# Attention scores by pairs of heads, each head on 64 of TensorE's rows

## The chip, the cores and the metric

The kernel runs on one core of a Trainium2 chip. The metric is the time of one execution on the device, in microseconds (us). Before the change three runs gave a median of 867.17 us, between 867.12 and 867.3. Beside the runs there is one profiled execution, from which all durations below are taken.

The engines of the core are named as the profile names them: PE is TensorE (matmuls; PEld its weight loads, which overlap), DVE is VectorE, ACT is ScalarE, POOL is GpSimd, and SP only issues DMAs. TensorE writes its results to PSUM, eight banks of 512 float32 columns on 128 partitions; DVE and ACT read them from there.

## The reference

One layer of a hybrid encoder on a sequence of 512 frames with a model width of 1024: an RMS norm, one wide projection, an attention branch and a recurrent branch, a gated merge, a SwiGLU feed-forward part and a final norm, all in float32. Only the attention branch is touched here. It has 16 heads of 64 features:

```python
q, k, v = ...                       # 512 x 1024 each, columns of xn @ w_in
s = einsum('bnqhd,bnkhd->bhnqk', q, kb) * (1 / 8)
s = s + rel_bias_band(rel_table)    # per head, on the clipped relative distance
s = where(valid, s, -1e30)          # chunks of 64 frames, own chunk and the 8 before it
p = softmax(s)
o = einsum('bhnqk,bnkhd->bnqhd', p, vb)
ya = o @ w_attn_out
```

With 512 frames there are eight chunks, so the band of nine chunks means: each frame sees its own chunk of 64 and everything before it.

## The kernel before

**Products in parts.** Every float32 operand x is kept as a high part (fp32r, written by ACT with a copy) and a low part (x minus the high part, written by DVE): `split`, line 80. A projection multiplies by `mm3`, line 74: high by high, high by low, low by high, three matmuls into one PSUM bank. `project` (line 342) does this for the eight slices of 128 of the contraction, so one tile of 128 output features by 512 frames is 24 matmuls.

**PSUM.** Three tags share the eight banks: `mm` has four, `s` two, `t` two. A tile of the program is one bank.

**Order.** Everything is traced in program order into a planner, which puts each engine's instructions in an order by its own simulation, and sets the semaphores from what each instruction reads and writes. Within `tc.manual_schedule(engines={PE})` (line 973) TensorE keeps the order in which the program names its instructions; DVE, ACT, POOL and SP are still ordered by the planner there. The loop over heads of the attention lies inside this block; the scores of the first head lie before it, among the products of `yb` (line 967 to 972).

**A pair's q and k.** Columns of w_in come in chunks `qk0` to `qk7`, 128 columns of q and 128 of k for a pair of heads, and `v0` to `v3` for four heads each. `q_tile` (line 834) projects q for a pair, features on partitions: head e of the pair has rows 64e to 64e+63. It writes the high part of the head into its own 64 rows of a tile and the low part into the other 64 rows (lines 841 and 842, for each head), so that a contraction over all 128 rows gives (high + low) times whatever stands in the 128 rows of the other operand. `k_tile` (line 845) makes two such operands for each head: the high part in both halves of the rows (lines 852 and 854) and the low part in both halves (853 by DVE, then a copy by POOL, 855).

**A head's scores** (`scores`, line 879). Frames are turned within blocks of 128, so that block qb of 128 queries needs the first (qb+1)*128 keys: 128, 256, 384 and 512 columns. `products(qb)` is two matmuls over 128 rows, q with the high part of k (line 895) and with the low part (896). Block 0 writes columns 0 to 127 and block 1 columns 256 to 511 of the same bank (`low`); blocks 2 and 3 have a bank each. In the program products(0) and products(1) both come before block 0 is read, products(2) before block 1 is read, and so on. Reading a block is line 904: DVE takes scores and bias from PSUM and SBUF, writes bias minus scores to SBUF and its minimum per row to `nmax` (the DVE_READ_ACCUMULATOR2 row beside it). ACT then takes the exponential with its row sum (905). The four reciprocals are one DVE instruction (906), and the four blocks are scaled by POOL, for three of the heads the last block by DVE (910).

**The other steps of a head.** `transposed` (913): ten 128 by 128 transposes by TensorE into three banks, which are split into high and low parts. `weigh` (930): eight matmuls of v with these, gathered into `oacc` by ACT and DVE (942, 943); after the second head of a pair the result is split into `aT`, the input of the projection `ya`.

**The loop** (lines 974 to 983) does, for head h: transposed(h), scores(h+1), a part of what is laid out by `laid(h)`, weigh(h), the rest of it. `laid` gives q and k of the pair after next, and v of the next four heads, in the order of the chunks; for the last four heads the products of `gate`. In the first iteration q and k of pair 1 come after scores(1), and are first used by scores(2) in the iteration after it.

Of the kernel before, what the change touches and what calls it, by code (L numbers as in the profile page):

```python
# [14 lines left out]
P = 128  # L15
# [23 lines left out]
def block_kernel(ctx: ExitStack, tc: tile.TileContext, x, norm_mix_g, w_in, b_merge, rel_table,  # L39
# [22 lines left out]
    qk_stack, qkp = opened("qk", 3, "right")  # L62
# [455 lines left out]
    def junk_of(pl, tag, bufs, name):  # L518
        return pl.tile([P, D], F32, tag=tag, bufs=bufs, name=f"junk_{name}")

    def rstds(half):

        q = cp.tile([P, 4], F32, tag="ssq", bufs=4, name=f"ssq{half}")
        sd = cp.tile([P, 2], F32, tag="sd", bufs=4, name=f"sd_mix{half}")
        rs = cp.tile([P, 2], F32, tag="rs", bufs=4, name=f"rs_mix{half}")
        a, b = xt[2 * half], xt[2 * half + 1]
        junk = junk_of(nm, "junk", 1, f"a{half}")
        act.activation(junk[:], a[:], AF.Square, accum_out=q[:, 0:1])
        act.activation(sd[:, 0:1], q[:, 0:1], AF.Sqrt, bias=eps_t[:], scale=1.0 / D)
# [3 lines left out]
        junk = junk_of(qkp, "qk", 3, f"c{half}")  # L533
# [287 lines left out]
    def backwards(ap):  # L821
        return blocks(ap)[:, :, ::-1]

    def halves(e):
        own, other = slice(e * HD, e * HD + HD), slice(HD - e * HD, 2 * HD - e * HD)
        return own, other


    qk = {}

    def qk_pool(pr):
        return aw if pr % 2 else qkp

    def q_tile(pr):
        po = mm_tile(f"po_q{pr}")
        project(po, weights(f"qk{pr}"), 0, xnT)
        q = qk_pool(pr).tile([P, 2, S], F32R, tag="qk", bufs=3, name=f"q{pr}")
        for e in range(2):
            own, other = halves(e)
            src = backwards(po[own, :])  # L840
            act.activation(blocks(q[own, e]), src, AF.Copy, scale=0.125)
            dve.scalar_tensor_tensor(blocks(q[other, e]), src, 0.125, blocks(f(q[own, e])), ALU.mult, ALU.subtract)
        qk[pr] = [q]

    def k_tile(pr):
        po = mm_tile(f"po_k{pr}")
        project(po, weights(f"qk{pr}"), 1, xnT)
        kh = qk_pool(pr).tile([P, 2, S], F32R, tag="qk", bufs=3, name=f"kh{pr}")
        kl = qk_pool(pr).tile([P, 2, S], F32R, tag="qk", bufs=3, name=f"kl{pr}")
        for e in range(2):  # L850
            own, other = halves(e)
            act.activation(kh[own, e], po[own, :], AF.Copy)
            dve.tensor_sub(kl[own, e], po[own, :], f(kh[own, e]))
            act.activation(kh[other, e], po[own, :], AF.Copy)
            pool.tensor_copy(kl[other, e], kl[own, e])
        qk[pr] += [kh, kl]

    q_tile(0)
    k_tile(0)
# [16 lines left out]
        vs.setdefault(gr, []).append(v)  # L876


    def scores(h):
        pr, e = divmod(h, 2)  # L880
        q, kh, kl = qk[pr]
        bias = bias_tile(h)
        lsum = cp.tile([P, NT], F32, tag="lsum", bufs=2, name=f"l{h}")
        nmax = cp.tile([P, NT], F32, tag="nmax", bufs=2, name=f"m{h}")
        rl = cp.tile([P, NT], F32, tag="rl", bufs=2, name=f"rl{h}")
        prob = [aw2.tile([P, (qb + 1) * P], F32, tag=f"p{qb}", name=f"p{h}_{qb}") for qb in range(NT)]

        low = ps.tile([P, S], F32, tag="s", bufs=2, name=f"s{h}_01")
        scs = [low[:, 0:P], low[:, 256:512], mm_tile(f"s{h}_2"), ps.tile([P, S], F32, tag="s", bufs=2, name=f"s{h}_3")]

        def products(qb):
            w = (qb + 1) * P
            sc = scs[qb][:, 0:w]
            qs = q[:, e, qb * P:(qb + 1) * P]
            pe.matmul(sc, qs, kh[:, e, 0:w], start=True, stop=False, skip_group_check=qb < 2)
            pe.matmul(sc, qs, kl[:, e, 0:w], start=False, stop=True, skip_group_check=qb < 2)  # L896

        products(0)
        for qb in range(NT):
            w = (qb + 1) * P  # L900
            if qb < NT - 1:
                products(qb + 1)

            dve.tensor_tensor_reduce(prob[qb][:], scs[qb][:, 0:w], bias[:, S - w:S], -1.0, 3e38, ALU.add, ALU.min, nmax[:, qb:qb + 1])  # L904
            act.activation(prob[qb][:], prob[qb][:], AF.Exp, bias=nmax[:, qb:qb + 1], scale=-1.0, accum_out=lsum[:, qb:qb + 1])  # L905
        dve.reciprocal(rl[:], lsum[:])  # L906
        for qb in range(NT):

            eng = dve if qb == NT - 1 and h % 4 == 1 and h > 1 else pool
            eng.tensor_scalar(prob[qb][:], prob[qb][:], rl[:, qb:qb + 1], 1.0, ALU.mult, ALU.mult)  # L910
        return prob

    def transposed(h, prob):

        pp = [aw2.tile([P, 2, S], F32R, tag="pt", bufs=4, name=f"pp{h}_{i}") for i in range(3)]
        for i, kbs in enumerate(((0,), (1,), (2, 3))):
            pt = mm_tile(f"pT{h}_{i}") if i == 2 else ps.tile([P, S], F32, tag="t", bufs=2, name=f"pT{h}_{i}")
            for kb in kbs:
                for qb in range(kb, NT):
                    at = qb - min(kb, 2) if kb < 3 else 2  # L920
                    pe.transpose(pt[:, at * P:(at + 1) * P], prob[qb][:, kb * P:(kb + 1) * P], ident[:])  # L921
            n = (512, 384, 384)[i]
            split(pp[i][:, 0, 0:n], pp[i][:, 1, 0:n], pt[:, 0:n])
        return pp

    aT = []
    aT_pairs = []
    oacc = []

    def weigh(h, pp):  # L930
        pr, e = divmod(h, 2)
        own, other = halves(e)
        if e == 0:
            oacc.append(tg_.tile([P, S], F32, tag="tg", name=f"oacc{pr}"))
        acc = oacc[pr]
        po = mm_tile(f"o{h}")
        for kb in range(NT):
            i, lo, n = ((0, 0, 512), (1, 0, 384), (2, 0, 256), (2, 256, 128))[kb]
            st = vs[pr // 2][kb][:, pr % 2, 2 * e:2 * e + 2].rearrange("p a d -> p (a d)")
            for part in range(2):  # L940
                pe.matmul(po[:, S - n:S], st, pp[i][:, part, lo:lo + n], start=kb == 0 and part == 0, stop=kb == NT - 1 and part == 1)  # L941
        act.activation(acc[own, :], po[other, :], AF.Copy)
        dve.tensor_add(acc[own, :], po[own, :], acc[own, :])
        if e == 1:
            if pr % 2 == 0:
                aT_pairs.append(rnp.tile([P, 2, 2, S], F32R, tag="big", bufs=4, name=f"aT{pr}"))
            o = aT_pairs[-1][:, pr % 2]
            split(blocks(o[:, 0]), blocks(o[:, 1]), backwards(acc[:]))
            aT.append(o)

    def laid(h):
        m, at = divmod(h, 4)
        qs, ks, va = (lambda pr: lambda: q_tile(pr)), (lambda pr: lambda: k_tile(pr)), (lambda t: lambda: v_tile(m + 1, t))
        if h >= 12:
            return [lambda: gate(0, h - 8)], []
        first_, second = 2 * m + 2, 2 * m + 3
        return {0: (([qs(1), ks(1)] if m == 0 else []) + ([] if m == 0 else [qs(first_)]), [qs(first_)] if m == 0 else []),
                1: ([ks(first_)], [va(0)]),  # L960
                2: ([va(1), va(2)], [va(3)]),
                3: ([qs(second)], [ks(second)])}[at]

    for t in range(NT):
        v_tile(0, t)
# [5 lines left out]
        project(po, weights(f"yb{j - j % 2}"), j % 2, rnn)  # L971
        dve.scalar_tensor_tensor(zB[j], zB[j], 1.0, po[:], ALU.add, ALU.mult)
    with tc.manual_schedule(engines={mybir.EngineType.PE}):
        for h in range(HEADS):
            pp = transposed(h, prob)
            if h + 1 < HEADS:
                prob = scores(h + 1)
            before, after = laid(h)
            for what in before:
                what()  # L980
            weigh(h, pp)
            for what in after:
                what()
    aw2_stack.close()
    wo_stack, wop = opened("wo", 4)
    extra["wo1"] = wop
# [373 lines left out]
```

## Time and profile before

| what | value |
|---|---|
| median of three runs | 867.17 us |
| span of the profiled execution, first to last instruction | 865.5 us |
| PE busy | 856.4 us, 99% of the span |
| DVE busy | 600.9 us, 69% |
| ACT busy | 498.1 us, 58% |
| POOL busy | 95.2 us, 11% |
| mean granted clock of TensorE | 0.998 |
| DMA | 96.39 MB, mean 111 GB/s |

The profiled execution has no time of its own beside its span; the median lies 1.67 us above it, for what lies ahead of the first and behind the last instruction.

How to read the rows: a row of a timeline gives the start in us from the start of the span, the duration in us, the engine, the line of the program, the operation, the tiles as out<-in, the shape, and how many instructions were merged (x1 is one). In brackets stands how long the engine had been idle before it, and what ended that. Matmuls overlap: each lasts longer than the distance to the next one's start, and it is this distance that adds up to the time of TensorE. A row that groups instructions gives their busy time and the mean duration of one in ns. A row of waits gives who waited for whom, the sum in us, how often, and sometimes the longest.

### The profile page before, as it was taken

Reading aid. Unit: us, or ns where it says so; the run is one execution under the profiler, and the core shown is the slowest. Engines: PE = TensorE matmul, PEld = TensorE weight load, DVE = VectorE, ACT = ScalarE, POOL = GpSimd, SP = SyncE. Lnnn points to the kernel's source line nnn. Section 1 sums busy time; section 2 is a strip of 40 time slices with the busy share of each in tenths; the row PEclk is TensorE's granted clock in tenths of the full one; section 3 lists DMA queues with packets and bytes.
Section 4 is the critical chain, followed back from the end, with each engine's and each line's share of the span. In section 5 each row is a group of like instructions: output and inputs, shape, how many; then the busy total and the mean of one; then the engine's idle time right before and its main releaser. Section 6 shows DMA issues by size and latency. Waiting matters only on the chain.

```text
span 865.5 us, 13353 instructions
## 1 busy us (share of the span) xinstructions
PE 856.4 (99%) x5130; PEld 761.1 (88%) x5130; DVE 600.9 (69%) x950; ACT 498.1 (58%) x878; POOL 95.2 (11%) x161
## 2 busy tenths in 40 slices
PE   9999999999999999999999999999999999999997
PEld 6988888888889889898888889999999999888885
DVE  5666656573456585766556556988888888698885
ACT  6595747752356585767633357555555556545434
POOL 2412111120112132221200000000000001000000
PEclk9999999999999999999999999999999999999999
DMA  9133232433323332232223712424333332437542
GB/s 289 57 119 106 68 120 76 123 98 98 109 88 95 81 103 74 81 113 64 74 76 121 266 51 72 145 79 131 109 98 98 99 98 85 148 100 227 185 134 97
DMA packets 88767, 96.39 MB, mean 111 GB/s; under 512 B 5784, under 2 KB 74992, under 8 KB 88704
## 3 DMA queue, kind: packets, MB, share of 16 engines
q1 hardware_dynamic: 87072, 92.03, 34.3%
q10 hardware_dynamic: 1232, 2.95, 0.9%
q8 instruction: 40, 0.66, 0.3%
q0 software_dynamic: 400, 0.57, 0.2%
q14 instruction: 23, 0.19, 0.1%
HBM read 93.39 MB, written 2.14 MB: 110 GB/s over the span
## 4 chain that ended last, share of the span: by engine, by line
PE 97%; DVE 1%; ACT 1%; DMA 0%; issue 0%; ACTq 0%; DVEq 0%
PE po_out L76 2%; PE po_out L77 2%; PE po_out L78 2%; PE o L941 2%; PE p_fu L78 2%; PE p_fg L78 2%; PE p_fg L77 2%; PE p_fg L76 2%; PE p_fu L76 2%; PE p_fu L77 2%; PE pT L921 2%; PE po_v L76 2%; PE po_v L78 2%; PE po_v L77 2%; PE po_gb L76 2%; PE po_xr L77 2%
## 5 line engine op out<-in xcount | busy, mean ns | idle before, releaser
L910 POOL TENSOR_SCALAR p<-p,rl 128x128 f32<-128x128 f32 (+3 forms) x61 | 34.9, 590 | 135.7 <-DVE rl L906 135.4
L905 ACT ACTIVATE p<-p,m 128x128 f32<-128x128 f32 (+1 forms) x64 | 35.7, 560 | 11.0 <-DVE m L904 10.8
L76 PE MATMUL po_v<-whl_v,xnT 128*128 128x256 f32 x128 | 36.5, 285 | 0.0
L78 PE MATMUL po_v<-whl_v,xnT 128*128 128x256 f32 x128 | 36.2, 283 | 0.0
L77 PE MATMUL po_v<-whl_v,xnT 128*128 128x256 f32 x128 | 36.2, 283 | 0.0
L1131 POOL TENSOR_TENSOR act_lo<-act,act_hi 128x1024 fp32r<-128x1024 f32 x1 | 2.4, 2405 | 300.7 <-ACT act_hi L1130 300.7
L76 PE MATMUL po_out<-whl_fo,act_hi 128*128 128x512 f32 (+1 forms) x80 | 30.8, 385 | 0.5 <-ACT c_u L370 0.5
L78 PE MATMUL po_out<-whl_fo,act_lo 128*128 128x512 f32 (+1 forms) x80 | 30.7, 384 | 0.0
L77 PE MATMUL po_out<-whl_fo,act_hi 128*128 128x512 f32 (+1 forms) x80 | 30.7, 384 | 0.0
L904 DVE CUSTOM_DVE_ANT_0 p<-s,bias 128x128 f32<-128x128 f32 (+1 forms) x64 | 29.1, 483 | 1.0 <-PE s L896 1.0
L83 DVE TENSOR_TENSOR whl_qk<-raw_qk,whl_qk 128x1024 fp32r<-128x1024 f32 x16 | 20.5, 1284 | 13.2 <-ACT whl_qk L82 13.0
L83 DVE TENSOR_TENSOR whl_fu_s<-s_fu,whl_fu_s 128x1024 fp32r<-128x1024 f32 x20 | 24.1, 1222 | 6.2 <-ACT whl_fu_s L82 6.2
L77 PE MATMUL po_xr<-xnT,whl_xr 128*128 128x512 f32 (+1 forms) x80 | 27.7, 353 | 0.0
L83 DVE TENSOR_TENSOR pp<-pT,pp 128x384 fp32r<-128x384 f32 (+1 forms) x48 | 27.5, 596 | 0.1
L77 PE MATMUL po_gr<-xnT,whl_gr 128*128 128x512 f32 (+1 forms) x80 | 27.5, 347 | 0.0
L78 PE MATMUL po_gr<-xnT,whl_gr 128*128 128x512 f32 (+1 forms) x80 | 27.3, 347 | 0.0
L78 PE MATMUL po_xr<-xnT,whl_xr 128*128 128x512 f32 (+1 forms) x80 | 27.2, 346 | 0.0
L76 PE MATMUL po_gr<-xnT,whl_gr 128*128 128x512 f32 (+1 forms) x80 | 27.2, 347 | 0.0
L83 DVE TENSOR_TENSOR whl_fg_s<-s_fg,whl_fg_s 128x1024 fp32r<-128x1024 f32 x20 | 24.0, 1222 | 4.1 <-ACT whl_fg_s L82 4.0
L76 PE MATMUL po_xr<-xnT,whl_xr 128*128 128x512 f32 (+1 forms) x80 | 26.3, 351 | 0.4 <-ACT xnT L566 0.4
L82 ACT ACTIVATE whl_qk<-raw_qk 128x1024 fp32r<-128x1024 f32 x16 | 16.8, 1053 | 17.0 <-PE po_yb L78 10.4
L76 PE MATMUL po_gb<-xnT,whl_gb 128*128 128x512 f32 x64 | 25.2, 394 | 0.0
(487 smaller groups left out, 3247.5 us busy)
## 6 DMA issues: line engine op xcount, KB each, us to landing
raw_fg<-in_w_ffn_in_dram SPq DMA_DIRECT2D x24, 512.0 KB, 4.2
raw_fu<-in_w_ffn_in_dram SPq DMA_DIRECT2D x22, 512.0 KB, 3.9
raw_qk<-in_w_in_dram SPq DMA_DIRECT2D x32, 256.0 KB, 3.2
raw_fo<-in_w_ffn_out_dram SPq DMA_DIRECT2D x16, 512.0 KB, 3.6
raw_xr<-in_w_in_dram SPq DMA_DIRECT2D x8, 512.0 KB, 4.3
raw_gr<-in_w_in_dram SPq DMA_DIRECT2D x8, 512.0 KB, 3.6
raw_ga<-in_w_in_dram SPq DMA_DIRECT2D x8, 512.0 KB, 4.7
raw_gb<-in_w_in_dram SPq DMA_DIRECT2D x8, 512.0 KB, 3.5
```

Source lines behind the costliest of these rows:

```text
L76: pe.matmul(o, sh, mh, start=start, stop=False, skip_group_check=parts)
L77: pe.matmul(o, sh, ml, start=False, stop=False, skip_group_check=parts)
L78: pe.matmul(o, sl, mh, start=False, stop=stop, skip_group_check=parts)
L82: act.activation(hi, src, AF.Copy)
L83: dve.tensor_sub(lo, src, f(hi))
L904: dve.tensor_tensor_reduce(prob[qb][:], scs[qb][:, 0:w], bias[:, S - w:S], -1.0, 3e38, ALU.add, ALU.min, nmax[:, qb:qb + 1])
L905: act.activation(prob[qb][:], prob[qb][:], AF.Exp, bias=nmax[:, qb:qb + 1], scale=-1.0, accum_out=lsum[:, qb:qb + 1])
L910: eng.tensor_scalar(prob[qb][:], prob[qb][:], rl[:, qb:qb + 1], 1.0, ALU.mult, ALU.mult)
L921: pe.transpose(pt[:, at * P:(at + 1) * P], prob[qb][:, kb * P:(kb + 1) * P], ident[:])
L941: pe.matmul(po[:, S - n:S], st, pp[i][:, part, lo:lo + n], start=kb == 0 and part == 0, stop=kb == NT - 1 and part == 1)
L1131: (dve if i else pool).tensor_sub(lo[:], o[:], f(hi[:]))
```

## The change

A pair of heads is now one unit. The tile of q holds the high part of both heads (each on its own 64 rows) and, beside it, the low part; the tile of k likewise. No part is written twice any more, and POOL copies nothing. A head's product is three matmuls over its 64 rows: q high with k high, q high with k low, q low with k high. Those of head 0 (rows 0 to 63) and head 1 (rows 64 to 127) follow each other in turn, each head into a bank of its own. For a pair and a block there are six matmuls of 64 rows where there were four of 128.

The scores of a pair take six banks: `low` of both heads from tag `s`, `mid` (block 2) from `t`, `last` (block 3) from `mm`. In the program the order is now products(qb) and at once the reading of block qb for both heads, then products(qb+1). The loop runs over eight pairs: for pair pr it does scores(pr+1), q of pair pr+2 and one tile of v, transposed(pr) for both heads, k of pair pr+2 and one more tile of v, weigh(pr) for both heads. In its first iteration q and k of pair 1 come ahead of scores(1). Scaling by the reciprocal is left wholly to POOL. The tiles of q and k have two buffers instead of three, the probabilities four instead of two, and the transposed parts get tags of their own by size.

```diff
     def q_tile(pr):
         po = mm_tile(f"po_q{pr}")
         project(po, weights(f"qk{pr}"), 0, xnT)
-        q = qk_pool(pr).tile([P, 2, S], F32R, tag="qk", bufs=3, name=f"q{pr}")
-        for e in range(2):
-            own, other = halves(e)
-            src = backwards(po[own, :])
-            act.activation(blocks(q[own, e]), src, AF.Copy, scale=0.125)
-            dve.scalar_tensor_tensor(blocks(q[other, e]), src, 0.125, blocks(f(q[own, e])), ALU.mult, ALU.subtract)
+        q = qk_tile(pr, "q")
+        src = backwards(po[:])
+        act.activation(blocks(q[:, 0]), src, AF.Copy, scale=0.125)
+        dve.scalar_tensor_tensor(blocks(q[:, 1]), src, 0.125, blocks(f(q[:, 0])), ALU.mult, ALU.subtract)
         qk[pr] = [q]
 
     def k_tile(pr):
         po = mm_tile(f"po_k{pr}")
         project(po, weights(f"qk{pr}"), 1, xnT)
-        kh = qk_pool(pr).tile([P, 2, S], F32R, tag="qk", bufs=3, name=f"kh{pr}")
-        kl = qk_pool(pr).tile([P, 2, S], F32R, tag="qk", bufs=3, name=f"kl{pr}")
-        for e in range(2):
-            own, other = halves(e)
-            act.activation(kh[own, e], po[own, :], AF.Copy)
-            dve.tensor_sub(kl[own, e], po[own, :], f(kh[own, e]))
-            act.activation(kh[other, e], po[own, :], AF.Copy)
-            pool.tensor_copy(kl[other, e], kl[own, e])
-        qk[pr] += [kh, kl]
+        k = qk_tile(pr, "k")
+        split(k[:, 0], k[:, 1], po[:])
+        qk[pr].append(k)
...
-    def scores(h):
...
+    def scores(pr):
+        q, k = qk[pr]
+        bias = [bias_tile(2 * pr + e) for e in range(2)]
...
+        low = [ps.tile([P, S], F32, tag="s", bufs=2, name=f"s{pr}_{e}_01") for e in range(2)]
+        mid = [ps.tile([P, S], F32, tag="t", bufs=2, name=f"s{pr}_{e}_2") for e in range(2)]
+        last = [mm_tile(f"s{pr}_{e}_3") for e in range(2)]
+        scs = [[low[e][:, 0:P], low[e][:, 256:512], mid[e][:, 0:3 * P], last[e][:]] for e in range(2)]
 
         def products(qb):
             w = (qb + 1) * P
-            sc = scs[qb][:, 0:w]
-            qs = q[:, e, qb * P:(qb + 1) * P]
-            pe.matmul(sc, qs, kh[:, e, 0:w], start=True, stop=False, skip_group_check=qb < 2)
-            pe.matmul(sc, qs, kl[:, e, 0:w], start=False, stop=True, skip_group_check=qb < 2)
-
-        products(0)
+            at = slice(qb * P, (qb + 1) * P)
+            for n, (qp, kp) in enumerate(((0, 0), (0, 1), (1, 0))):
+                for e in range(2):
+                    rows = half_of(e)
+                    pe.matmul(scs[e][qb], q[rows, qp, at], k[rows, kp, 0:w], start=n == 0, stop=n == 2,
+                              skip_group_check=qb < 2)
+
+        def weighted(qb, e):
+            p, n = prob[e][qb], stat[e]
+            at = slice(qb, qb + 1)
+            dve.tensor_tensor_reduce(p[:], scs[e][qb], bias[e][:, S - (qb + 1) * P:S], -1.0, 3e38, ALU.add, ALU.min,
+                                     n["nmax"][:, at])
+            act.activation(p[:], p[:], AF.Exp, bias=n["nmax"][:, at], scale=-1.0, accum_out=n["lsum"][:, at])
+
         for qb in range(NT):
-            w = (qb + 1) * P
-            if qb < NT - 1:
-                products(qb + 1)
-
-            dve.tensor_tensor_reduce(prob[qb][:], scs[qb][:, 0:w], bias[:, S - w:S], -1.0, 3e38, ALU.add, ALU.min, nmax[:, qb:qb + 1])
...
+            products(qb)
+            for e in range(2):
+                weighted(qb, e)
...
+    def laid(pr):
+        if pr >= 6:
+            return [], [lambda: gate(0, 2 * pr - 8)], [lambda: gate(0, 2 * pr - 7)]
+        m, at = divmod(pr, 2)
+        qs, ks, va = (lambda p: lambda: q_tile(p)), (lambda p: lambda: k_tile(p)), (lambda t: lambda: v_tile(m + 1, t))
+        return ([qs(1), ks(1)] if pr == 0 else [], [qs(pr + 2), va(2 * at)], [ks(pr + 2), va(2 * at + 1)])
...
     with tc.manual_schedule(engines={mybir.EngineType.PE}):
-        for h in range(HEADS):
-            pp = transposed(h, prob)
-            if h + 1 < HEADS:
-                prob = scores(h + 1)
-            before, after = laid(h)
-            for what in before:
+        for pr in range(HEADS // 2):
+            first_, second, third = laid(pr)
+            for what in first_:
                 what()
-            weigh(h, pp)
-            for what in after:
+            ahead = scores(pr + 1) if pr + 1 < HEADS // 2 else None
+            for what in second:
                 what()
+            pp = transposed(pr, prob)
+            for what in third:
+                what()
+            weigh(pr, pp)
+            prob = ahead
```

More of the change, by code (lines that the diff above doesn't have):

```diff
@@ L822, in backwards, with half_of, qk_tile @@
         return blocks(ap)[:, :, ::-1]
[L824 to L826 removed]
+    def half_of(e):
+        return slice(e * HD, e * HD + HD)
     qk = {}
[L831 to L832 removed]
+    def qk_tile(pr, name):
+        return (aw if pr % 2 else qkp).tile([P, 2, S], F32R, tag="qk", bufs=2, name=f"{name}{pr}")
     def q_tile(pr):
@@ L926, in block_kernel @@
     aT = []
     aT_pairs = []
[L928 to L949, printed above, removed]
@@ L953, in laid, with weigh @@
[L953 to L962, printed above, removed]
+    def weigh(pr, pps):
+        acc = tg_.tile([P, S], F32, tag="tg", name=f"oacc{pr}")
+        for e, pp in enumerate(pps):
+            own, other = half_of(e), half_of(1 - e)
+            po = mm_tile(f"o{pr}_{e}")
+            for kb in range(NT):
+                i, lo, n = ((0, 0, 512), (1, 0, 384), (2, 0, 256), (2, 256, 128))[kb]
+                st = vs[pr // 2][kb][:, pr % 2, 2 * e:2 * e + 2].rearrange("p a d -> p (a d)")
+                for part in range(2):
+                    pe.matmul(po[:, S - n:S], st, pp[i][:, part, lo:lo + n], start=kb == part == 0,
+                              stop=kb == NT - 1 and part == 1)
+            act.activation(acc[own, :], po[other, :], AF.Copy)
+            dve.tensor_add(acc[own, :], po[own, :], acc[own, :])
+        if pr % 2 == 0:
+            aT_pairs.append(rnp.tile([P, 2, 2, S], F32R, tag="big", bufs=4, name=f"aT{pr}"))
+        o = aT_pairs[-1][:, pr % 2]
+        split(blocks(o[:, 0]), blocks(o[:, 1]), backwards(acc[:]))
+        aT.append(o)
```

54 lines of the change are left out of this document (27 added, 27 removed).

## Prediction

> **What bounds the kernel now.** First the page: busy shares, and the chain of work that ended last.
>
> ```profile
> PE 856.4 (99%) x5130; PEld 761.1 (88%) x5130; DVE 600.9 (69%) x950; ACT 498.1 (58%) x878; POOL 95.2 (11%) x161
> PE 97%; DVE 1%; ACT 1%; DMA 0%; issue 0%; ACTq 0%; DVEq 0%
> ```
>
> TensorE is busy for 99% of the span and is 97% of the chain. A busy PE could still hide slack, so next the waits of PE over the whole span, and the stretch of the attention (229 to 436 us) by engine.
>
> ```profile
> PE busy L396 <- DVE eps_t L402: 1.2, 1, 1.2
> PE pt_mix_0t L564 <- DVE xs_mix L544: 0.6, 2, 0.4
> PE po_out L76 <- ACT c_u L370: 0.5, 1, 0.5
> PE po_xr L76 <- ACT xnT L566: 0.4, 2, 0.2
> ```
> ```profile
> 229.00:436.00 207.00, 207.00 (x1209) 183.84 (x1208) 134.24 (x290) 133.36 (x286) 46.98 (x89) 1.00 0.31 90
> ```
>
> None of the four waits lies in the attention: there PE waits for nobody, while DVE is busy for 134.24 of 207 us (65%) and ACT for 133.36. So in this stretch a product saved is time saved, a product added is time lost, and a new wait of PE is paid in full. Work taken from ACT, DVE or POOL is worth nothing by itself.
>
> **The scores now.** One head (the sixth) as the timeline has it:
>
> ```profile
> 301.40 0.30 PE L895 MATMUL s<-kh,q 128*128 128x128 f32 x1
> 301.54 0.28 PE L896 MATMUL s<-kl,q 128*128 128x128 f32 x1
> 301.66 0.33 PE L895 MATMUL s<-kh,q 128*128 128x256 f32 x1
> 301.83 0.28 PE L896 MATMUL s<-kl,q 128*128 128x256 f32 x1
> 301.94 0.34 PE L895 MATMUL s<-kh,q 128*128 128x384 f32 x1
> 302.12 0.33 PE L896 MATMUL s<-kl,q 128*128 128x384 f32 x1
> 302.24 0.29 DVE L904 CUSTOM_DVE_ANT_0 p<-s,bias 128x128 f32<-128x128 f32 x1 [0.34 <-PE s L896]
> 302.29 0.39 PE L895 MATMUL s<-kh,q 128*128 128x512 f32 x1
> 302.46 0.08 DVE L904 DVE_READ_ACCUMULATOR2_ANT m<- 128x1 f32 x1
> 302.46 0.42 DVE L904 CUSTOM_DVE_ANT_0 p<-s,bias 128x256 f32<-128x256 f32 x1
> 302.52 0.40 PE L896 MATMUL s<-kl,q 128*128 128x512 f32 x1
> 302.75 0.40 PE L76 MATMUL po_q<-xnT,whl_qk 128*128 128x512 f32 x1
> 302.80 1.22 DVE L83 TENSOR_TENSOR whl_v<-raw_v,whl_v 128x1024 fp32r<-128x1024 f32 x1
> ```
>
> From the first product to the next other one: 302.75 - 301.40 = 1.35 us, 2.70 for a pair of heads. The distances from one start to the next, by width: 0.12 at 128 columns (301.54), 0.11 at 256 (301.83), 0.17 at 384 (302.12), 0.23 at 512 (302.52).
>
> **The scores after.** Each block takes three pairs of 64-row products. The kernel has such pairs already, in the gates of the recurrent branch (line 709, twelve products, two row halves in turn):
>
> ```profile
> 47.20 0.39 PE L78 MATMUL po_ga<-xnT,whl_ga 128*128 128x512 f32 x1
> 47.52 1.66 PE L709 MATMUL rg<-xch,wrg 64*128 64x512 f32 x12
> 49.11 0.50 PE L76 MATMUL po_gb<-xnT,whl_gb 128*128 128x512 f32 x1
> 49.45 0.40 PE L77 MATMUL po_gb<-xnT,whl_gb 128*128 128x512 f32 x1
> ```
>
> The last whole-array product starts at 47.20 and owes 0.23, so the twelve take 49.11 - 47.43 = 1.68. Twelve after each other would be 2.76, six pairs 1.38: the halves do run beside each other, with 0.30 more for going into that mode and out. The first product behind takes 0.34 instead of 0.23, another 0.11. So a visit costs 0.41. Narrower pairs do not occur; I take the distances above, since a pair's two weight loads also run beside each other there. For a pair of heads: 3 x (0.12 + 0.11 + 0.17 + 0.23) + 0.41 = 2.30, against 2.70. Eight pairs: 3.2 us gained. If narrow pairs were no better than two products in turn at 128 and 256 columns, each pair of heads would pay 3 x 0.23 = 0.69 more and the gain would be a loss of 2.3; I keep the gain, because the row with pairs is the nearest, and hold the loss for the range.
>
> [...]
>
> **The wait that the new order makes.** Blocks 0 and 1 of a head share a bank. Before, both were computed before block 0 was read. In the rows above block 0 is complete at 301.54 + 0.28 = 301.82, yet DVE, idle for 0.34, reads it only at 302.24: 0.13 after block 1 is complete (301.83 + 0.28 = 302.11). Its next read, of block 1, starts with no wait. So the planner orders by the bank, not by the columns. The same holds between readers, in the evacuation of q:
>
> ```profile
> 249.19 0.39 PE L78 MATMUL po_q<-xnT,whl_qk 128*128 128x512 f32 x1
> 249.61 0.59 ACT L841 ACTIVATE q<-po_q 64x512 fp32r<-64x512 f32 x1 [1.88 <-PE po_q L78]
> 250.23 0.68 DVE L842 SCALAR_TENSOR_TENSOR q<-po_q,q 64x512 fp32r<-64x512 f32 x1 [2.29 <-ACT q L841]
> 250.95 0.59 ACT L841 ACTIVATE q<-po_q 64x512 fp32r<-64x512 f32 x1 [0.75 <-DVE q L842]
> ```
>
> ACT's second read (rows 64 to 127 of the bank, written to a place DVE doesn't use) stands until DVE has read rows 0 to 63. After the change the program names products(0), then both reads of block 0, then products(1) into the same banks. TensorE keeps program order in the loop, so by this rule it stops before block 1 until DVE has read block 0 of both heads, and all that PE has queued (blocks 1 to 3, q, v) stands behind it.
>
> No row shows a writer held by a reader of other columns, so the row alone leaves this open. [...]
>
> Its price: let s be the start of block 0's last product. Without a wait the next would start at s + 0.12. The product ends at s + 0.28, DVE reads head 0 from s + 0.41. Its second part starts 0.22 later (302.46) and lasts 0.08; head 1's read starts at s + 0.63, and is released at s + 0.93. From DVE's end to PE I take 0.05:
>
> ```profile
> 7.13 0.48 DVE L544 TENSOR_SCALAR xs_mix<-x,rs_mix 128x512 f32<-128x512 f32 x1
> 7.66 0.14 PEld L564 LDWEIGHTS pt_mix_0t<-ident,xs_mix 128*128 128x128 f32 x1 [0.47 <-DVE xs_mix L544]
> ```
>
> So head 1 goes on at s + 0.98: 0.86 lost if DVE is free. Mostly it is not:
>
> ```profile
> DVE p L904 <- PE s L896: 1.0, 3, 0.3
> ```
> ```profile
> 358.78 0.28 PE L896 MATMUL s<-kl,q 128*128 128x256 f32 x1
> 359.58 1.16 DVE L83 TENSOR_TENSOR pp<-pT,pp 128x512 fp32r<-128x512 f32 x2
> 360.66 0.28 DVE L904 CUSTOM_DVE_ANT_0 p<-s,bias 128x128 f32<-128x128 f32 x1
> ```
>
> Only for 3 of 16 heads did DVE stand waiting for scores; at the eleventh it read block 0 at 360.66, 1.47 later than it could (359.06 + 0.13). What was a backlog that nobody felt becomes PE's. I take 0.7, the middle of 0 and 1.47, since the scores will again follow weigh and evacuations on DVE. So 1.56 for each of the seven pairs in the loop: 10.9. The first pair's scores lie outside the loop, where the planner may put products of yb into the gap at the price of another visit (0.41) or leave the 0.86: 0.6.
>
> **The first iteration.** q and k of pair 1 now come directly ahead of scores(1). From the rows of 249 us: product ends 0.39 after its start, ACT begins 0.03 later, takes 0.59, DVE begins 0.03 later and takes 0.68, PE 0.05 on. The pair that needs k's low part can start 1.77 after the last k product instead of 0.35: 1.4. If ACT and DVE were each at a weight conversion,
>
> ```profile
> L83 DVE TENSOR_TENSOR whl_qk<-raw_qk,whl_qk 128x1024 fp32r<-128x1024 f32 x14 | 18.1, 1292 | 12.7 <-ACT whl_qk L82 12.7
> L82 ACT ACTIVATE whl_qk<-raw_qk 128x1024 fp32r<-128x1024 f32 x13 | 13.7, 1053 | 9.9 <-issue 4.8 <-PE po_yb L78 3.3 <-PE po_v L78 1.8
> ```
>
> it would be 1.4 + 1.29 + 1.05 = 3.7. I take 1.9, near the lower end, since both stood idle (1.88, 2.29) in the same place at 249 us.
>
> **What I cost at nothing.** A pair's q and k evacuations fall from six ACT, four DVE and two POOL instructions to two, two and none: all off the path. The last blocks that DVE scaled go to POOL; the probabilities are used a whole iteration later. The six score banks are needed again by the transposes; q and v stand between, over 24 x 0.23 = 5.5 us, while DVE's eight reads take
>
> ```profile
> L904 DVE CUSTOM_DVE_ANT_0 p<-s,bias 128x128 f32<-128x128 f32 (+1 forms) x64 | 29.1, 483 | 1.0 <-PE s L896 1.0
> L904 DVE DVE_READ_ACCUMULATOR2_ANT m<- 128x1 f32 x64 | 5.3, 83 | 0.0
> ```
>
> (29.1 + 5.3) / 8 = 4.3, of which the last banks count; uncovered they would cost up to 4.3 for a pair. The splits before weigh have k and v (more than 5.5) as cover, likewise. On SP's queue both bias tiles of a pair come free together, an iteration ahead. The chunks of q/k and v now alternate, so a chunk's buffers come free when k or the last v is done; v, weigh and scores lie between that and the next q, about as much as the two conversions need.
>
> **The sum.** -3.2 + 10.9 + 0.6 + 1.9 = +10.2: span 875.7. The median is 867.17 for a span of 865.5, 1.67 above it; kept, this gives 877.4. Low end: DVE always free, -3.2 + 6.0 + 0.4 + 1.4 = +4.6, 871.8. High end: DVE late by 1.47 each time, -3.2 + 16.3 + 0.9 + 3.7 = +17.7, 884.9. The loss of 2.3 in place of the gain would add 5.5; that it falls together with the latest DVE is left to the little that the range leaves out.
>
> **Rivals.**
> *Block 1 doesn't wait* (other side). The place is the second block's first product; it decides whether the planner orders a write behind a read of other columns. For it: no row shows such a wait. Against: DVE and ACT do wait by the bank. Sum: -3.2 + 1.9 = -1.3, 865.9, within 0.2%; with the lower end of the first iteration 865.4.
> *A conversion falls between the two reads.* DVE puts 1.29 us of weight conversion between head 0's and head 1's read, as it put 1.22 behind the second read at 302.80 in the sixth head. For: DVE's order is the planner's. Against: the reads stood together in the rows above. 7 x 1.29 = 9.0 more: 886.4.
> *The halves don't run beside each other*, for instance since the four loads of narrow products collide. 12 x 0.63 / 4 = 1.89 for each pair of heads, 15.1 in all: 892.5. Against it are the rows at 47.52.
>
> **Chances.** The forecast 0.76 (872 to 885 by itself), no wait 0.12, conversion between 0.08, no overlap 0.04. A measurement tells 0.2% (1.7 us) from no change. Faster: 0.04, a third of the no-wait case, when the first iteration costs its least; same 0.08, the rest of it; slower 0.88. The range from 871 to 886.5 leaves out the no-wait case, the last one and little else.
>
> **What would show it.** Right: PE rows of the scores in 64-row form, 192 products; a gap of 1 to 2.5 us between block 0 and block 1 in each pair, ended by DVE p; a wait of PE on ACT or DVE k ahead of scores(1); PE busy share down by about a point; pairs of products 0.11 to 0.23 apart; DVE and ACT less busy than before. Wrong: PE dense through the scores, or a long gap before the transposes, before weigh or before q (a chunk not converted).

## The result and the profile after

The changed kernel takes 876.89 us (median of four runs, 876.14 to 877.79), the kernel before 867.2 us beside it. The ratio is 1.0112, with a 95% interval from 1.0097 to 1.0127: 9.69 us slower. The profiled execution has a span of 876.0 us against 865.5.

The profile is of the longest of the four, 877.79. The page after, in the order in which the prediction read it: busy shares, TensorE's granted clock by slice, the chain that ended last, and the group of the scores.

```profile
PE 861.5 (98%) x5194; PEld 760.6 (87%) x5194; DVE 586.1 (67%) x931; ACT 478.9 (55%) x846; POOL 80.2 (9%) x148
PEclk9999999999989999999999999999999999999999
PE 96%; DVE 2%; DMA 1%; ACT 1%; issue 1%; ACTq 0%; DVEq 0%
L889 PE MATMUL s<-k,q 64*128 64x128 f32 (+3 forms) x192 | 22.3, 354 | 5.6 <-DVE stats L895 4.5
```

DVE, ACT and POOL are all less busy, as forecast, and the kernel is slower. The waits of PE say why; these are those that the kernel before did not have in the attention.

```profile
PE s L889 <- DVE stats L895: 4.5, 7, 1.3
PE s L889 <- ACT k L82: 0.7, 1, 0.7
PE s L889 <- DVE k L83: 0.4, 1, 0.4
```

Seven waits on DVE's reading of the scores, one in each scores(pr) of the loop, and one each on the high and the low part of k. The same stretch by engine, in the columns that the prediction showed (PE, PEld, DVE, ACT, POOL, granted clock, DMA share, GB/s):

```profile
229.00:436.00 207.00, 201.37 (x1224) 174.77 (x1223) 115.28 (x268) 111.54 (x252) 34.64 (x78) 0.98 0.29 85
```

PE is no longer dense: 201.37 of 207 us, where it was 207.00. And the granted clock of this stretch is 0.98, where it was 1.00. This second difference is one that the prediction did not expect.

The scores of pair 2, as the timeline after has them:

```profile
283.26 0.55 PE L889 MATMUL s<-k,q 64*128 64x128 f32 x6
283.94 0.29 DVE L895 CUSTOM_DVE_ANT_0 p<-s,bias 128x128 f32<-128x128 f32 x1 [0.53 <-PE s L889]
284.16 0.08 DVE L895 DVE_READ_ACCUMULATOR2_ANT stats<- 128x1 f32 x1
284.16 0.29 DVE L895 CUSTOM_DVE_ANT_0 p<-s,bias 128x128 f32<-128x128 f32 x1
284.30 2.05 PE L889 MATMUL s<-k,q 64*128 64x256 f32 x18 [0.49 <-DVE stats L895]
284.38 0.08 DVE L895 DVE_READ_ACCUMULATOR2_ANT stats<- 128x1 f32 x1
286.28 0.50 PE L76 MATMUL po_q<-xnT,whl_qk 128*128 128x512 f32 x1
```

This is the forecast mechanism: the six products of block 0, DVE's read of head 0 until 284.24 (284.16 + 0.08), PE again 0.06 later; head 1 is released at 284.46. But DVE had been idle for 0.53 when block 0 came. It was not late. The same holds for pairs 4 and 6. In pairs 3, 5 and 7 DVE was at a gather of `oacc` behind a weight conversion and read 0.12 later; this is pair 3:

```profile
309.00 2.05 PE L889 MATMUL s<-k,q 64*128 64x256 f32 x18 [0.61 <-DVE stats L895]
```

The first iteration, and two of the products of q that follow its scores:

```profile
253.63 0.39 PE L78 MATMUL po_k<-xnT,whl_qk 128*128 128x512 f32 x1
254.06 0.60 ACT L82 ACTIVATE k<-po_k 128x512 fp32r<-128x512 f32 x1 [1.61 <-PE po_k L78]
254.69 0.69 DVE L83 TENSOR_TENSOR k<-po_k,k 128x512 fp32r<-128x512 f32 x1 [0.98 <-ACT k L82]
254.71 0.33 PE L889 MATMUL s<-k,q 64*128 64x128 f32 x2 [0.69 <-ACT k L82]
255.43 0.44 PE L889 MATMUL s<-k,q 64*128 64x128 f32 x4 [0.40 <-DVE k L83]
255.63 1.23 DVE L83 TENSOR_TENSOR whl_v<-raw_v,whl_v 128x1024 fp32r<-128x1024 f32 x1 [0.25 <-ACT whl_v L82]
256.77 0.28 DVE L895 CUSTOM_DVE_ANT_0 p<-s,bias 128x128 f32<-128x128 f32 x1
257.12 0.79 PE L889 MATMUL s<-k,q 64*128 64x256 f32 x2 [1.25 <-DVE stats L895]
```
```profile
261.10 0.63 PE L77 MATMUL po_q<-xnT,whl_qk 128*128 128x512 f32 x1
261.52 0.63 PE L78 MATMUL po_q<-xnT,whl_qk 128*128 128x512 f32 x1
```

PE stands for k's high part (0.69), for k's low part (0.40), and then for 1.25, because here, and only here, DVE was at a weight conversion (255.63, 1.23 long) when block 0 was complete. Behind it the products of q start 0.42 apart instead of 0.23. The windows of 4 us around this place say what that is:

```profile
254.00:258.00 4.00, 1.66 (x14) 1.36 (x15) 2.34 (x6) 2.42 (x6) 0.00 (x0) 0.79 0.46 133
258.00:262.00 4.00, 4.00 (x19) 3.06 (x18) 3.14 (x13) 3.25 (x11) 0.00 (x0) 0.50 0.44 129
262.00:266.00 4.00, 4.00 (x17) 3.28 (x16) 0.35 (x2) 0.66 (x2) 3.66 (x8) 0.86 0.43 131
```

PE was busy for 1.66 of 4 us, and the granted clock fell: 0.79 as a mean of these 4 us, 0.50 over the next 4. In the trace it stands at 0.50 from 256.31 to 263.14, for 6.83 us.

### The profile page after: what moved, and what is told of

It reads as the page before. It is cut to its first block, busy times and chain, and to the rows that moved or that the text cites. A ratio compares the mean times of both kernels' runs of the same rounds, so it can differ in the third digit from the quotient of the medians.

```text
span 876.0 us, 13339 instructions
## 1 busy us (share of the span) xinstructions
PE 861.5 (98%) x5194; PEld 760.6 (87%) x5194; DVE 586.1 (67%) x931; ACT 478.9 (55%) x846; POOL 80.2 (9%) x148
## 4 chain that ended last, share of the span: by engine, by line
PE 96%; DVE 2%; DMA 1%; ACT 1%; issue 1%; ACTq 0%; DVEq 0%
PE s L889 2%; PE po_out L76 2%; PE po_out L78 2%; PE po_out L77 2%; PE o L940 2%; PE p_fu L78 2%; PE p_fg L78 2%; PE p_fg L77 2%; PE p_fg L76 2%; PE p_fu L76 2%; PE p_fu L77 2%; PE pT L922 2%; PE po_q L76 2%; PE po_v L78 2%; PE po_v L77 2%; PE po_v L76 2%
## 5 line engine op out<-in xcount | busy, mean ns | idle before, releaser
L907 POOL TENSOR_SCALAR p<-p,stats 128x128 f32<-128x128 f32 (+1 forms) x64 | 32.8, 532 | 195.4 <-DVE stats L905 194.8
L897 ACT ACTIVATE p<-p,stats 128x128 f32<-128x128 f32 (+3 forms) x64 | 35.3, 553 | 6.2 <-DVE stats L895 6.1
L83 DVE TENSOR_TENSOR pp<-pT,pp 128x384 fp32r<-128x384 f32 (+1 forms) x48 | 25.2, 594 | 8.5 <-ACT pp L82 8.5
L895 DVE CUSTOM_DVE_ANT_0 p<-s,bias 128x128 f32<-128x128 f32 (+3 forms) x64 | 28.2, 486 | 3.2 <-PE s L889 2.9
L889 PE MATMUL s<-k,q 64*128 64x128 f32 (+3 forms) x192 | 22.3, 354 | 5.6 <-DVE stats L895 4.5
```

Of the source, the lines that this page charges most:

```text
L83: dve.tensor_sub(lo, src, f(hi))
L889: pe.matmul(scs[e][qb], q[rows, qp, at], k[rows, kp, 0:w], start=n == 0, stop=n == 2, skip_group_check=qb < 2)
L895: dve.tensor_tensor_reduce(p[:], scs[e][qb], bias[e][:, S - (qb + 1) * P:S], -1.0, 3e38, ALU.add, ALU.min, n["nmax"][:, at])
L897: act.activation(p[:], p[:], AF.Exp, bias=n["nmax"][:, at], scale=-1.0, accum_out=n["lsum"][:, at])
L907: pool.tensor_scalar(prob[e][qb][:], prob[e][qb][:], n["rl"][:, qb:qb + 1], 1.0, ALU.mult, ALU.mult)
```

## The experiments

The theory after the result: three losses, each with a place. The order products, reading, products stops PE at the shared bank; k directly ahead of scores(1) stops it once more; and these stops together let the clock fall. Against it stood the rivals of the prediction and others, named with each run. Each run was measured beside runs of the kernel before, whose median was 867.06 to 867.20; the ratio is to these. Edits are against the changed kernel unless said otherwise.

### The next block's products ahead of the reading

```diff
+        products(0)
         for qb in range(NT):
-            products(qb)
+            if qb < NT - 1:
+                products(qb + 1)
             for e in range(2):
                 weighted(qb, e)
```

> Block 1's products stand ahead of the reading of block 0 again, everything else as changed. Theory (the wait for the reading of block 0 in the shared bank is the main loss): no wait of PE on DVE in the scores; a pair in the loop takes 2.3 to 2.5 us instead of 3.13 to 3.26, six pairs give 4.5 to 5; pair 1 loses only the 1.5 for k; 867.5 if the clock then stays whole, 870.2 if it falls to half all the same. Rival (DVE itself is too slow for eight reads in a row, and the wait only moves to the next use of the banks): waits of like size ahead of the transposes or of q, 874 or more.

Measured: 866.75 us (866.56 to 867.65), ratio to the kernel before 0.9996 (0.9987 to 1.0005). No wait of PE on DVE's reading is left; the two for k are. The windows of the first iteration:

```profile
254.00:258.00 4.00, 2.91 (x27) 1.95 (x27) 2.77 (x10) 2.02 (x5) 0.00 (x0) 1.00 0.45 131
258.00:262.00 4.00, 4.00 (x18) 3.29 (x19) 2.75 (x13) 4.00 (x15) 0.32 (x1) 1.00 0.61 171
```

Two lines of the program's order carry 876.89 - 866.75 = 10.1 us, more than the whole loss, the half clock among it. With 2.91 of 4 us busy the clock stayed at 1.00.

### k of pair 1 earlier

q and k of pair 1 go ahead of the last products of yb, and no longer stand directly before scores(1).

```diff
-        return ([qs(1), ks(1)] if pr == 0 else [], [qs(pr + 2), va(2 * at)], [ks(pr + 2), va(2 * at + 1)])
+        return ([], [qs(pr + 2), va(2 * at)], [ks(pr + 2), va(2 * at + 1)])
...
+        if j == KT - 1:
+            q_tile(1)
+            k_tile(1)
```

> q and k of pair 1 are projected ahead of the last product of yb, everything else as changed (block 1 still waits). Theory (the two waits of the first iteration together, 1.5 for k and 1.4 at block 1, brought the clock to half): the 1.5 for k is gone, the granted clock stays at 1.00 behind scores(1), together 4 us: 872.7, and the runs lie closer together than 876.1 to 877.8. Rival (the clock falls because of the block wait or for a reason of its own): 875.4, with a stretch at 0.50.

Measured: 872.74 us (872.6 to 872.96), 1.0064 (1.0051 to 1.0077), 4.15 less than the changed kernel. The waits of PE, and the window of the first iteration:

```profile
PE s L889 <- DVE stats L895: 3.8, 7, 0.7
```
```profile
254.00:258.00 4.00, 3.49 (x29) 2.77 (x28) 4.00 (x15) 3.13 (x10) 0.00 (x0) 1.00 0.63 177
```

The seven waits remain, none longer than 0.7; those for k are gone and the clock stays whole.

### Both

The two edits above together.

> Both of these edits. Theory: no wait of PE in the attention, the clock whole, a pair of heads at 2.3 to 2.5 us against 2.55 before: 865.2 to 867.2. Rival (pairs of 64-row products are dearer than the rows of the gates say): above 868.

Measured: 865.55 us (865.38 to 866.1), 0.9983 (0.9974 to 0.9992): faster than both kernels, by 1.51 us against the 867.06 of the one before beside it. All scores of a pair now stand without a gap:

```profile
324.40 2.18 PE L889 MATMUL s<-k,q 64*128 64x128 f32 x24
325.85 0.29 DVE L895 CUSTOM_DVE_ANT_0 p<-s,bias 128x128 f32<-128x128 f32 x1
326.51 0.50 PE L76 MATMUL po_q<-xnT,whl_qk 128*128 128x512 f32 x1
```

From the first product to the next other one 2.11 us, and DVE's first read (325.85) begins 1.45 after the first product, while PE goes on.

### The same order, another bank

Block 1 goes into the bank of block 2, and block 2 into that of block 0. Order and reads are as in the changed kernel.

```diff
-        scs = [[low[e][:, 0:P], low[e][:, 256:512], mid[e][:, 0:3 * P], last[e][:]] for e in range(2)]
+        scs = [[low[e][:, 0:P], mid[e][:, 0:2 * P], low[e][:, P:S], last[e][:]] for e in range(2)]
...
-                              skip_group_check=qb < 2)
+                              skip_group_check=qb in (0, 2))
```

> The changed order stays (products of a block, at once its reading), but block 1 gets a bank of its own and block 2 (384 columns) shares the bank of block 0. Theory (the wait follows the shared bank): no wait ahead of block 1; one ahead of block 2 of 0.3 to 0.4 instead of 0.65 to 0.78, as block 1's products now lie in it; 873 to 875. Rival (a block waits for the reading of the block before it, whatever the bank): waits at block 1 as now, 876.9.

Measured: 872.81 us (871.87 to 874.27), 1.0066 (1.0053 to 1.008). The waits on the reading, and a later pair:

```profile
PE s L889 <- DVE stats L895: 1.6, 4, 0.8
```
```profile
355.30 0.95 PE L889 MATMUL s<-k,q 64*128 64x128 f32 x12
356.12 0.27 DVE L895 CUSTOM_DVE_ANT_0 p<-s,bias 128x128 f32<-128x128 f32 x1
356.33 0.28 DVE L895 CUSTOM_DVE_ANT_0 p<-s,bias 128x128 f32<-128x128 f32 x1
356.46 1.70 PE L889 MATMUL s<-k,q 64*128 64x384 f32 x12 [0.20 <-DVE stats L895]
```

Blocks 0 and 1 now follow each other without a stop (twelve products in one row), and PE stops ahead of block 2 instead, which writes the bank that DVE reads. So the wait goes to whichever block writes the bank that is being read, and the products of block 1 cover a part of it. A tile of the program is a bank here, and it is the planner that sets the wait, so the runs can't tell the bank from the tile. The clock fell here too (it stood at 0.50 for 3.41 us, from 258.66):

```profile
254.00:258.00 4.00, 2.07 (x18) 1.27 (x18) 2.76 (x10) 2.00 (x5) 0.00 (x0) 1.00 0.45 131
258.00:262.00 4.00, 4.00 (x18) 2.86 (x16) 2.85 (x13) 4.00 (x15) 0.31 (x1) 0.58 0.59 156
```

### Filling the wait with products that nobody needs

To measure the clock by itself: six products of 512 columns into a bank of their own, between k of pair 1 and scores(1). The bank is not read.

```diff
+            if pr == 0:
+                fill = mm_tile("fill")
+                for _ in range(6):
+                    pe.matmul(fill[:], xnT[0][:, 0, 0:P], xnT[0][:, 0], start=True, stop=True)
```

> The changed kernel with six useless 128x512 products (1.36 us) between k of pair 1 and scores(1), into a bank that nobody reads; k and block 1 are waited for as before. Theory (idle time of PE within a few us lowers the clock): the six lie in the wait for k, the granted clock stays at 1.00, and the time falls by 2.5 to 3 although work is added: 874. Rival (the clock falls for another reason, or the products only delay): 877 to 878.5.

Measured: 874.5 us (874.49 to 874.61), 1.0085 (1.0069 to 1.0102). Work was added, and the kernel became 2.39 us faster. The seven waits on DVE are as they were, the clock isn't:

```profile
PE s L889 <- DVE stats L895: 4.5, 7, 1.3
```
```profile
254.00:258.00 4.00, 2.75 (x23) 2.10 (x23) 2.54 (x7) 2.40 (x6) 0.00 (x0) 1.00 0.46 134
258.00:262.00 4.00, 4.00 (x24) 3.14 (x21) 2.93 (x13) 3.71 (x12) 0.36 (x2) 1.00 0.53 157
```

The runs lie 0.12 us apart at most; those of the changed kernel, 1.65, and those of the run with another bank, where the clock fell too, 2.40. In these three the scatter is larger where the clock fell. It is not so throughout: 1.09 with the next block's products ahead, where the clock stayed whole here, and 0.05 in the kernel before read at once (the next run), where it fell.

### The kernel before, read at once

The prediction took 0.7 us for each pair for a backlog of DVE. In the changed kernel DVE had next to none (0.53 idle at 283.94, 0.12 late in pair 3). Is it the order of the loop that does away with it, or was the backlog never felt? The kernel before with the order that makes the wait, and nothing else:

```diff
-        products(0)
         for qb in range(NT):
             w = (qb + 1) * P
-            if qb < NT - 1:
-                products(qb + 1)
+            products(qb)
```

> The kernel before, with one edit: products of a block and at once its reading, so that block 1 comes behind the reading of block 0. Fifteen heads lie in the loop. Theory A (the planner then puts the reading first on DVE, as it did in the changed kernel): a wait of about 0.65 for a head, 10 us: 877. Theory B (as the forecast had it: DVE's backlog before the first reading, 0.7 in the mean, stays and becomes PE's): 1.35 for a head, 20 us: 887. Rival (the wait belongs to the 64-row products): 867.

Measured: 886.26 us (886.24 to 886.29), 1.0221 (1.0206 to 1.0236). The waits, and one of them in the timeline:

```profile
PE s L895 <- DVE m L902: 14.3, 15, 1.8
```
```profile
315.89 0.28 PE L896 MATMUL s<-kl,q 128*128 128x128 f32 x1
316.26 0.69 DVE L842 SCALAR_TENSOR_TENSOR q<-po_q,q 64x512 fp32r<-64x512 f32 x1
316.98 0.69 DVE L83 TENSOR_TENSOR pp<-pT,pp 128x512 fp32r<-128x512 f32 x1
317.59 0.28 DVE L902 CUSTOM_DVE_ANT_0 p<-s,bias 128x128 f32<-128x128 f32 x1
317.94 0.38 PE L895 MATMUL s<-kh,q 128*128 128x256 f32 x1 [1.77 <-DVE m L902]
```

Fifteen waits, 14.3 us of the 19.1 by which it is slower. By the starts of the products they cost more, 16.8, since the next product would have begun before the one ahead of it had ended (0.12 behind its start, of 0.28). Another 1.7 (an estimate: half of 3.41 us) belong to the clock, which fell behind the wait shown, and not behind a like one with as little work around it:

```profile
316.00:320.00 4.00, 2.23 (x11) 1.81 (x11) 3.94 (x12) 2.74 (x9) 0.00 (x0) 0.90 0.00 0
320.00:324.00 4.00, 4.00 (x14) 3.20 (x13) 0.42 (x3) 1.52 (x5) 2.21 (x5) 0.68 0.21 66
368.00:372.00 4.00, 2.23 (x20) 2.07 (x18) 3.02 (x7) 2.94 (x7) 0.33 (x2) 1.00 0.00 0
```

The remaining 0.6 stay open. In the place shown, block 0 is complete at 316.17; DVE reads it 1.42 later, behind an evacuation of q and a split of the transposes. In the old loop the scores follow the transposes, whose splits are DVE's; in the new one they follow weigh of the pair before, or k and q, and DVE waits for them or is 0.12 late, but for pair 1. The backlog was real for nine of the fifteen heads (the other six wait 0.49, with DVE free), but it belongs to the old order, from whose rows the 0.7 was taken. Even there it comes to about 0.5 as a mean: 16.8 / 15 = 1.12 for a wait, against 0.65 for a free DVE.

### Head by head

Do the halves run beside each other because their products are named in turn? The kernel with both edits, with the two loops exchanged: three products of head 0, then three of head 1, for each block.

```diff
-            for n, (qp, kp) in enumerate(((0, 0), (0, 1), (1, 0))):
-                for e in range(2):
+            for e in range(2):
+                for n, (qp, kp) in enumerate(((0, 0), (0, 1), (1, 0))):
```

> As e3_both, but a block's three products of head 0 come first and those of head 1 behind them, instead of in turn. Theory (two row halves run beside each other only where neighbours in the order lie on different halves): of six products of a block two overlaps are left, at the changes of head, so four steps instead of three, 0.63 more for a pair of heads, 5 us in all: 870.6. Rival (order makes no difference, the halves run ahead by themselves): 865.6. Rival (no overlap is left): 12 x 0.63 / 4 = 1.9 for a pair, 880.7.

Measured: 865.69 us (865.55 to 866.4), 0.9985 (0.9975 to 0.9994). My theory was wrong.

```profile
325.23 2.19 PE L889 MATMUL s<-k,q 64*128 64x128 f32 x24
327.35 0.50 PE L76 MATMUL po_q<-xnT,whl_qk 128*128 128x512 f32 x1
```

2.12 us, as with products in turn. How far does that go? All twelve products of head 0, then all twelve of head 1, and only then the reading (again against the kernel with both edits):

```diff
-        def products(qb):
+        def products(qb, e):
...
-                for e in range(2):
-                    rows = half_of(e)
+                for rows in (half_of(e),):
...
-        products(0)
+        for e in range(2):
+            for qb in range(NT):
+                products(qb, e)
         for qb in range(NT):
-            if qb < NT - 1:
-                products(qb + 1)
             for e in range(2):
                 weighted(qb, e)
```

> As e3_both, but all twelve products of head 0 come first in the order, then all twelve of head 1, then the readings. Theory (each row half takes its products from the queue by itself, as the run by heads within a block showed for three): if it reaches twelve ahead, no change, 865.6; if it reaches only a few ahead, the rest stands in line: up to 1.9 for a pair of heads, 15 in all, 880.7.

Measured: 874.7 us (874.62 to 874.81), 1.0087 (1.0069 to 1.0105).

```profile
329.08 3.33 PE L888 MATMUL s<-k,q 64*128 64x128 f32 x24
332.34 0.50 PE L76 MATMUL po_q<-xnT,whl_qk 128*128 128x512 f32 x1
```

3.26 us for a pair, 1.15 more; by eight 9.2, and 9.15 were measured against the kernel with both edits. The starts (us) of single products in this pair, from the same trace:

```
330.231  384 columns, the ninth of one head
330.238  128 columns, the first of the other
330.406  512 columns, the tenth of the first head
330.635  512 columns, the eleventh
330.869  512 columns, the twelfth
```

The other head's first product starts when three of the first head's, which the program names before it, have not yet started.

## Why the prediction came out as it did

877.4 was forecast, 876.89 measured, and the mechanism that it named as the main one is there. But the total is nearer than its terms, and that is luck. The runs form a chain in which each step takes away one thing, and whose differences add up to the measured 9.69:

| step | from one run to the next | measured, us | forecast, us |
|---|---|---|---|
| half clock | 876.89 to 874.50, useless products added | +2.39 | none |
| wait for k ahead of scores(1) | 874.50 to 872.74, k earlier | +1.76 | +1.9 |
| reading before the next products | 872.74 to 865.55 | +7.19 | +10.9 and +0.6 |
| paired products of 64 rows | 865.55 to 867.20, the kernel before | -1.65 | -3.2 |
| sum | | +9.69 | +10.2 |

The first row is a difference of medians. Against 874.50 the four runs lost 1.64, 1.81, 2.98 and 3.29 us, with a mean granted clock of 0.997, 0.996, 0.995 and 0.995. The profile, which is of the last, has the half clock for 6.83 us, twice the 3.41 of the run with another bank; that the first two had it half as long is an estimate from their losses (half of 3.41 is 1.7), there is no trace of them. The useless products are six of 0.23, 1.36 us in all by their starts, and fill a wait of 1.37, so this step is nearly pure.

The second row is not. In the traces it is 2.07 from the first score product to the last (177.29 us with the useless products, 175.21 with k earlier): about 1.36 in the place of the wait for k, and 0.76 because the long wait of pair 1 (1.25 at 257.12) shrinks to that of the others. The difference to 1.76 lies outside this stretch and was not traced. So its nearness to the 1.9 is luck too. In the third row the traces give the same 7.19 as the medians (175.21 - 168.02); with the 0.76 of pair 1 the reading cost 7.95. The last row is against the 867.20 of the first comparison; beside the run itself it was 1.51.

*The gain of the pairs.* For the new side the step holds: 2.11 us from the first score product to the next other one, which then takes 326.84 - 326.51 = 0.33 instead of 0.23. The first product also starts late behind weigh's last one: 0.20 after it, where a whole-array product follows after 0.11 (both by the starts in the traces), so 0.09. This makes 2.11 + 0.10 + 0.09 = 2.30, the forecast itself, and 2.30 - 1.89 puts a visit to the 64-row mode at 0.41, as in the gates. One after another, by the distances of whole-array products, the 24 would take 2 x 1.89 = 3.78. So running beside each other is worth a factor of 3.78 / 2.30 = 1.6 here, the 0.41 included. Wrong was the old side, 2.70 for two heads. The row ahead of the scores that the prediction showed is

```profile
300.72 0.93 PE L921 MATMUL pT<-ident,p 128*128 128x128 f32 x7
```

The last transpose starts at 300.72 + 0.93 - 0.28 = 301.37, and transposes are (0.93 - 0.28) / 6 = 0.11 apart. The first score product, at 301.40, comes 0.03 behind it, so 0.08 of the 1.35 belongs to the transpose. Two heads took 2.55, and the gain is about 0.25 for a pair, 2.0 in all, where 1.65 was measured; the rest was not traced. Narrow pairs being no better than products in turn did not come to pass, nor did the halves fail to overlap, the third rival.

*The wait at the shared bank.* Right in place, cause and number: one in each of seven pairs, at block 1, ended by DVE's read, and gone to block 2 when the bank changes. The rival in which block 1 doesn't wait fell with the first profile. The rows before had shown an order by the bank only for reads (0.34 of DVE at 302.24, 0.75 of ACT at 250.95); that a write is held by a read of other columns too was the author's estimate, and the trace shows that the planner does so (0.49 idle at 284.30). What the hardware does where the two meet, no run here shows. Mis-sized was its price. The 0.86 for a DVE that is free is about right in sum, though not in its parts: block 0's last product starts at 283.26 + 0.55 - 0.28 = 283.53, the next would at 283.65 and does at 284.30, 0.65 later; the rest is that head 0 restarts one read of DVE earlier than head 1 (284.30 and 284.52), so that the halves run out of step for a while: 286.28 - 284.30 = 1.98 for blocks 1 to 3, which take 1.72 without the wait (324.78 to 326.51). From the first score product to the next other one it is 3.02 here against 2.11, so 0.91, and 0.97 as a mean over six pairs. The step that failed is the 0.7 of backlog, put on each pair: it was nothing in pairs 2, 4 and 6, where DVE stood idle ahead of the scores, and 0.12 in pairs 3, 5 and 7. Only pair 1 met a backlog of that size, 0.76, directly behind one weight conversion (1.25 of waiting). So the second rival, a conversion that delays the reads of every pair, came true once and not seven times, and ahead of the two reads, not between them.

*The first pair.* The planner did put products of yb between the blocks of scores(0), for a second visit: 0.42 more than one visit by the starts in the trace, against 0.6.

*The first iteration.* The wait for k came as described: 0.85 and 0.61 beyond the due starts, 1.46 together, of which 0.09 is the visit's, against a lower end of 1.4 and 1.9 taken. It was the lower end. ACT and DVE were idle, as at 249 us.

*What was left out.* The half clock, 2.39 us, is a term that the prediction put at nothing without a reason. It worked out each wait in microseconds of standing still and took every product behind it at full speed.

*Costed at nothing.* Evacuations of q and k, POOL's scaling, banks for the transposes, splits before weigh, the bias, the chunks: no wait of PE on any of these appeared. In the same 207 us DVE had 134.24 - 115.28 = 19 us less work and ACT 22 (the changed kernel gets a little less far in them), and with both edits, where PE waits for nobody there, it was the 1.65 us of TensorE that counted.

So, by the rows of the table, a loss of 4.3 too much (10.9 and 0.6 against 7.19), a gain of 1.55 too much and a clock that was missing made a total that is 0.5 off: errors that cancelled. The runs bear out the direction and the cause, not the sum.

## What to carry to other kernels

Where TensorE is the bound, name the next products into a bank before the reading of what lies in it, or put neighbouring blocks into different banks (four waits of 1.6 us in all instead of seven of 4.5); here a saving of 1.65 us was bought with 7.19 of such waits. A backlog of another engine has to be taken from the order of work that the change makes, not from that of the kernel before. And where waits of TensorE lie close together, count its busy share over some 4 us and not only the waits: with 1.66 and 2.07 of 4 us, and in one of two places with 2.23, the products behind them ran at a granted clock of 0.50 for a while (0.42 us apart instead of 0.23 in the changed kernel); with 2.75 and more in the same place it stayed at 1.00.

## What the runs showed of the hardware

**Waits of at most 1.25 us, close together, went with half the clock.** In the first iteration of the changed kernel PE stood for 0.69, 0.40 and 1.25 us, no longer at a time, yet with PE busy for 1.66 of 4 us the granted clock was 0.50 in the next 4, and with 2.07 of 4 (another bank) it was 0.58. At 2.75, 2.91 and 3.49 in the same place it stayed at 1.00. At 2.23 of 4, around a wait of 1.77 in the kernel before read at once, it fell once (316 us) and once not (368 us), so the busy share of such a window alone does not decide. The half clock lasted 3.41 us in two runs and 6.83 in the changed kernel. Where the limit lies, and over what time it counts, these runs leave open. Useless products in the wait for k, with the seven waits on DVE as they were (4.5 us), kept it at 1.00 and made the kernel 2.39 us faster.

**The two halves of the rows did not keep the program's order between them.** In the last run a product of 128 columns of head 1 starts at 330.238, and three of head 0 named before it start from 330.406 on. Naming the heads' products three and three instead of in turn made no difference (865.69 against 865.55), while twelve and twelve cost 9.15 us. What sets the three was not tried.
